# First FFN matrix as 2 x 2 blocks in seven products, six FFN phases, the residual in a DRAM scratch

## The chip, the core and the metric

The kernel runs on one core of one Trainium2 chip. The metric is the device time in microseconds (us) of one execution. Engines: TensorE (PE) multiplies, VectorE (DVE) and ScalarE (ACT) work element by element, GpSimd (POOL) builds masks, SyncE (SP) issues the transfers (DMA).

## What is computed

One layer of a hybrid encoder on 640 rows (512 of a prompt, 128 of eight samples) of 1024 columns in fp32: three token mixers on one normalised input, an attention to a memory, and a SwiGLU feed-forward part (FFN). The change is in the last.

```python
def swiglu(h, w_in, w_out):                    # h: rows x 1024, w_in: 1024 x 5632, w_out: 2816 x 1024
    g, u = jnp.split(h @ w_in, 2, axis=-1)
    return (jax.nn.silu(g) * u) @ w_out

h = rmsnorm(x, p['norm_ffn_pre'][l])
x = x + rmsnorm(swiglu(h, p['w_ffn_in'][l], p['w_ffn_out'][l]), p['norm_ffn_post'][l]).astype(x.dtype)
```

## The kernel before

Each fp32 operand of a large product is split into two parts (`split`): h, a cast by ACT to the type fp32r, and l, the rest, a subtraction by DVE. A product then is three matmuls, h by h, h by l and l by h, for each 128 of the contraction; they add up in one PSUM bank. Weights go through `ring`: a raw slot (three of them, `load_raw`), an h slot and an l slot (four of each). The slots have the size of the widest chunk, 4 x 278 columns. PSUM has eight banks, two for each of the tags g, t, z and o.

The order of the work on each engine is made by a planner from the priority in the program's text and from what is ready; the program only says what depends on what.

The stages in order: first norm; natural projections (`proj_nat`, seven chunks of 276 or 278 columns, the first two as rows arrive, three as fill of the stick-breaking attention, two as fill of the gated linear attention); that attention; gates and branch projections (`branch`, 320 columns); output projection with residual and next norm (`ProjD`, class with `start` for the first 512 columns and `finish` for the rest); memory attention; its output projection (`xo`, the same class); FFN.

`ProjD.finish` takes the tiles of 128 rows in turn: products, square sum, residual X, norm (`normed`, into a buffer of its own), and two tiles later the transposes (`done`). The last two calls of `done` are returned as `behind`. For `xo` they write fT_h and fT_l, the activations of the FFN transposed: 1024 channels by 640 rows.

The FFN (`ffn_phase`) has two phases of 11 x 128 hidden channels. A unit (`ffn_unit`, `ffn_load`) is 128 gate and the matching 128 up channels: 8 contraction tiles x 3 products for each, first for 384 rows, then for 256 (PARTS). ACT applies Silu to the gate's bank, DVE multiplies with the up's bank, and the result is split into ga or gb. In the first phase the first two units run their 384-row halves first, with `behind[0]` and `behind[1]` after them, and then their 256-row halves. After the 11 units come the products with the second matrix (L1199 to L1201), 512 columns at a time, for five tiles of rows; phase 0 copies the banks to Y, phase 1 adds Y and does the last norm, the residual and the stores (`finish`, L1217 to L1235).

Of the kernel before, what the change touches and what calls it, by code (L numbers as in the profile page):

```python
# [33 lines left out]
def tile_hybrid_stream_step(  # L34
# [27 lines left out]
    # ---------------------------------------------------------------- helpers  # L62
# [56 lines left out]
    def gemm_nat(ps, xh, xl, t0, slots, c0, cw, late=None, mid=None):  # L119
        """one tile of rows by cw columns"""  # L120
# [9 lines left out]
    def gemm_T(ps, slots, c0, xh, xl, t0, n, late=None):  # L130
        """128 columns by n rows, transposed"""
# [40 lines left out]
    def transposed(xn):  # L172
        """8 blocks of 128 columns, transposed, in two banks"""
# [13 lines left out]
    def normed(wpool, src, gain, bufs=2):  # L187
        """rmsnorm of 128 natural rows, by halves of the columns"""
        xn = wpool.tile([P, D], F32, tag="xn", bufs=bufs, name="xn")
# [33 lines left out]
    # ---------------------------------------------------------------- first norm  # L223
# [3 lines left out]
    widths = [276] * 5 + [278] * 2  # L227
# [21 lines left out]
    # products that keep the clock of the tensor engine up until the first rows are there  # L249
# [26 lines left out]
    # masks (functions of the shapes alone)  # L276
# [43 lines left out]
    # ---------------------------------------------------------------- pools of the mixer phase  # L320
# [24 lines left out]
    # natural projections: v of the stick-breaking heads, then q, k, low-rank input, v, gate of the linear attention  # L345
# [16 lines left out]
    # the first two chunks tile by tile, as the rows arrive  # L362
# [3 lines left out]
    # ---------------------------------------------------------------- projection u, pooling branch  # L366
# [21 lines left out]
    # pooling branch  # L388
# [36 lines left out]
    # pool state of the prompt (last 15 tokens) and of the samples (last 15 of 16 tokens)  # L425
# [13 lines left out]
    # q, k of the stick-breaking heads (transposed), v (natural), low-rank gate input  # L439
# [13 lines left out]
    # new keys and values of the stick-breaking heads  # L453
# [14 lines left out]
    # ---------------------------------------------------------------- stick-breaking attention  # L468
# [10 lines left out]
    def stick(z, t, m, n):  # L479
        """exp(z - sum of t over this and the later keys), m blocks of n keys"""  # L480
# [17 lines left out]
    def sb_prompt_a(i, hs):  # L498
        """weights of the heads hs for the queries of tile i, transposed"""
# [128 lines left out]
    # ---------------------------------------------------------------- gated linear attention  # L628
# [6 lines left out]
    def gla_prep(i):  # L635
        """transposed q, k, decay sums, and decayed keys of tile i"""
# [11 lines left out]
        # log decay (times tau)  # L648
# [12 lines left out]
        # running sums, transposed; remaining sums, natural  # L661
# [21 lines left out]
    def gla_main(i, pre, S):  # L683
# [6 lines left out]
        # attention inside the tile  # L690
# [5 lines left out]
        for hh in levels:  # L696
            nb = 64 // hh
            nk = P - hh  # no key is later than this
# [23 lines left out]
        # queries against the state  # L722
# [48 lines left out]
        # norm per head, output gate  # L771
# [18 lines left out]
    for c in range(5, 7):  # L790
        proj_nat(c)
# [9 lines left out]
    # ---------------------------------------------------------------- gates and branch projections  # L801
# [46 lines left out]
    # ---------------------------------------------------------------- output projection of the mixer  # L848
# [7 lines left out]
    class ProjD:  # L856
        """X += rmsnorm(x @ w) * gain, by tiles of rows: start(i) the first half of the columns, finish() the rest;
        done(i, rmsnorm(X) * gain2) for each tile of rows,
        two tiles behind; the last two calls are returned"""
# [17 lines left out]
        def finish(self, wpool, gain2, done):  # L877
            self.ws = load_w512(self.w2d, 512, 512, self.name + "1")
            xns = []
            for i in range(NT):  # L880
                self.unit(i, 1, (lambda: done(i - 2, xns[i - 2])) if i > 1 else None)
# [3 lines left out]
                for cs in (slice(0, 512), slice(512, D)):  # L885
                    nc.vector.scalar_tensor_tensor(X[:, i, cs], self.Y[:, i, cs], r, X[:, i, cs], ALU.mult, ALU.add)
                xns.append(normed(wpool, X[:, i, :], gain2, 3))
            return [lambda i=i: done(i, xns[i]) for i in (NT - 2, NT - 1)]
# [16 lines left out]
    # ---------------------------------------------------------------- cross-attention  # L905
# [6 lines left out]
    def proj_q():  # L912
        """all transposed products of the weight chunks; the first two run by groups of rows, as those arrive"""
# [50 lines left out]
    def softmax(ps, n):  # L964
        """n blocks of 256 columns of ps, normalised, into SBUF"""
# [13 lines left out]
    def xs_load(b):  # L979
        """cached keys of sample b, transposed, and values"""  # L980
# [48 lines left out]
    # keys and values of the prompt's memory  # L1029
# [48 lines left out]
    # the samples, between the products for the prompt's memory  # L1078
# [14 lines left out]
    # the prompt, between the products of the output projection  # L1093
# [22 lines left out]

    fpool = open_pool("fpool")
    nx = open_pool("nx", "right")
# [11 lines left out]
    def open_fw():  # L1130
        fw = open_pool("fw", "right")
        return fw, gain_tile(fw, norm_ffn_post, "gpost")

    fw = g_post = None

    def ffn_phase(ph):
        nonlocal fw, g_post
        ga_h = hpool.tile([P, KT, TOK], F32R, tag="th", name="ga_h")
        ga_l = hpool.tile([P, KT, TOK], F32R, tag="tl", name="ga_l")

        def gt(k):
            return (ga_h[:, k], ga_l[:, k]) if k < 8 else (gb_h[:, k - 8], gb_l[:, k - 8])
        def ffn_load(k):
            c0 = (ph * 11 + k) * P
            return load_w8(w1, [(c0, P), (FF + c0, P)], f"f{ph}_{k}", None)

        def ffn_unit(k, ws, half):
            dh, dl = gt(k)
            t0, n = PARTS[half]
            sl = slice(t0, t0 + n)  # L1150
            pg = bank([P, n], "g", "pg")
            gemm_T(pg, ws, 0, fT_h, fT_l, t0, n, 1 if ph == 0 and k < 2 else None)
            s = fpool.tile([P, PARTS[0][1]], F32, tag="sl", bufs=3, name="s")[:, 0:n]
            nc.scalar.activation(s, pg, AF.Silu)  # L1154
            pu = bank([P, n], "t", "pu")
            gemm_T(pu, ws, P, fT_h, fT_l, t0, n, 1 if ph == 0 and k < 2 else None)
            nc.vector.tensor_tensor(s, pu, s, ALU.mult)  # L1157
            split(dh[:, sl], dl[:, sl], s)
        w0 = [ffn_load(k) for k in range(2)]
        for half in range(2):  # L1160
            for k in range(2):
                ffn_unit(k, w0[k], half)
                if ph == 0 and half == 0:
                    behind[k]()
            if ph == 0 and half == 0:
                nx.release()
                nw.release()
                fw, g_post = open_fw()
        gb_h = fw.tile([P, 3, TOK], F32R, tag="gb_h", name="gb_h")
        gb_l = fw.tile([P, 3, TOK], F32R, tag="gb_l", name="gb_l")  # L1170
        for k in range(2, 11):
            ws = ffn_load(k)
            for half in range(2):
                ffn_unit(k, ws, half)
# [110 lines left out]
```

## Time and profile before

| | us |
|---|---|
| median of 3 runs | 1336.32 |
| lowest and highest | 1333.74, 1336.38 |
| span of the profiled execution | 1332.9 |
| PE busy | 1313.9 (99%) |
| DVE busy | 629.3 (47%) |
| ACT busy | 541.5 (41%) |

The median is 3.4 us above the span of the profiled execution. A duration in a row is that of one instruction from start to end; PE's instructions overlap, so their distance from start to start is shorter than their duration. Rows with x4 or x8 put that many consecutive instructions together.

### The profile page before, as it was taken

The numbers are of one execution on the slowest core, as the hardware profiler recorded it, in microseconds if no ns is written. First come the engines' busy times: TensorE is split into PE (matmuls) and PEld (weight loads), VectorE is DVE, ScalarE is ACT, GpSimd is POOL, SyncE is SP. The second block draws the span as 40 slices with busy tenths as digits, with TensorE's granted clock in tenths as the row PEclk, the third lists the DMA queues.
The fourth block names the chain that finished last, engine by engine and source line by source line (L and its number), as shares of the span: only waits on it lengthen the run. The fifth ranks groups of instructions, "written<-read, shape, count | busy, mean of one in ns | idle before, by whom it ended". The sixth has DMA issues, their size and how long they took to land.

```text
span 1332.9 us, 21503 instructions
## 1 busy us (share of the span) xinstructions
PE 1313.9 (99%) x8754; PEld 1194.7 (90%) x8754; DVE 629.3 (47%) x1242; ACT 541.5 (41%) x1087; POOL 41.3 (3%) x162
## 2 busy tenths in 40 slices
PE   9999999999999999999999999999999999999997
PEld 8998678988999999979988878899999889999986
DVE  6434775485587454547444434742322112322235
ACT  5324665454353454435444523642222222322222
POOL 2001111001000000000000000000000000000000
PEclk9999999999999999999999999999999999999999
DMA  7324231202412222422368821232222223232212
GB/s 233 112 77 128 82 97 49 60 1 66 116 30 68 84 88 75 144 94 95 127 227 296 270 79 33 70 105 64 84 75 72 72 73 86 64 95 64 75 52 79
DMA packets 134296, 128.65 MB, mean 97 GB/s; under 512 B 15670, under 2 KB 116613, under 8 KB 134197
## 3 DMA queue, kind: packets, MB, share of 16 engines
q1 hardware_dynamic: 133909, 126.98, 30.7%
q8 instruction: 69, 1.13, 0.3%
q0 software_dynamic: 288, 0.29, 0.1%
q14 instruction: 30, 0.25, 0.1%
HBM read 119.10 MB, written 8.15 MB: 95 GB/s over the span
## 4 chain that ended last, share of the span: by engine, by line
PE 93%; DVE 3%; DMA 2%; ACT 1%; issue 0%; SPq 0%; POOL 0%; DVEq 0%; ACTq 0%
PE ps_g L114 12%; PE pu L114 12%; PE pg L114 12%; PE ps_d L114 8%; PE ps_n L114 7%; PE ps_xq L114 4%; PE ps_b L114 4%; PE acc L1201 4%; PE acc L1199 4%; PE acc L1200 4%; PE ps_qk L114 3%; PE pl L718 2%; PE ps_xk L114 2%; PE ps_xv L114 1%; PE z L505 1%; PE xo L1074 1%
## 5 line engine op out<-in xcount | busy, mean ns | idle before, releaser
L1157 DVE TENSOR_TENSOR s<-pu,s 128x384 f32<-128x384 f32 (+1 forms) x44 | 21.5, 488 | 125.2 <-PE pu L114 125.2
L1199 PE MATMUL acc<-wh_o,ga_h 128*128 128x512 f32 (+1 forms) x168 | 64.5, 384 | 0.0
L1201 PE MATMUL acc<-wh_o,ga_l 128*128 128x512 f32 (+1 forms) x168 | 64.4, 384 | 0.0
L1200 PE MATMUL acc<-wl_o,ga_h 128*128 128x512 f32 (+1 forms) x168 | 64.3, 382 | 0.0
L89 DVE TENSOR_TENSOR wl_o<-raw_o,wh_o 128x1024 fp32r<-128x1024 f32 (+1 forms) x24 | 27.2, 1135 | 77.7 <-ACT wh_o L83 77.5
L1154 ACT ACTIVATE s<-pg 128x384 f32<-128x384 f32 (+1 forms) x44 | 19.3, 439 | 89.6 <-PE pg L114 89.6
L813 ACT ACTIVATE sgm<-ps_g 128x320 f32<-128x320 f32 x48 | 21.0, 437 | 66.0 <-PE ps_g L114 65.9
L83 ACT CAST wh_o<-raw_o 128x1024 fp32r<-128x1024 f32 (+1 forms) x24 | 23.5, 978 | 49.8 <-PE acc L1201 36.7
L143 ACT CAST ga_h<-s 128x384 fp32r<-128x384 f32 (+1 forms) x32 | 14.7, 459 | 63.2 <-DVE s L1157 63.2
L1201 PEld LDWEIGHTS acc<-wh_o,ga_l 128*128 128x128 f32 x168 | 31.5, 188 | 6.8
L1200 PEld LDWEIGHTS acc<-wl_o,ga_h 128*128 128x128 f32 x168 | 31.6, 188 | 6.7
L1199 PEld LDWEIGHTS acc<-wh_o,ga_h 128*128 128x128 f32 x168 | 31.5, 188 | 6.5
L718 PEld LDWEIGHTS pl<-X 96*120 96x120 f32 (+6 forms) x256 | 28.9, 181 | 6.4 <-issue 3.7
L814 DVE TENSOR_SCALAR sgm<-sgm 128x320 f32<-128x320 f32 x48 | 15.5, 325 | 40.4 <-ACT sgm L813 40.3
L718 PE MATMUL pl<-X 96*120 96x64 f32 (+6 forms) x256 | 30.5, 263 | 2.8 <-DVE X L714 2.7
L114 PE MATMUL ps_d<-wh_xo,oT_h 128*128 128x512 f32 x80 | 32.4, 405 | 0.0
L114 PE MATMUL ps_d<-wh_mix,mT_h 128*128 128x512 f32 x80 | 31.9, 398 | 0.0
L114 PE MATMUL ps_d<-wl_xo,oT_h 128*128 128x512 f32 x80 | 31.7, 396 | 0.0
L114 PE MATMUL ps_d<-wh_xo,oT_l 128*128 128x512 f32 x80 | 31.6, 396 | 0.0
L114 PE MATMUL ps_d<-wl_mix,mT_h 128*128 128x512 f32 x80 | 31.6, 395 | 0.0
L114 PE MATMUL ps_d<-wh_mix,mT_l 128*128 128x512 f32 x80 | 31.4, 392 | 0.0
L815 ACT ACTIVATE sgm<-sgm 128x320 f32<-128x320 f32 x48 | 22.5, 469 | 15.8 <-DVE sgm L814 15.7
(1207 smaller groups left out, 4442.1 us busy)
## 6 DMA issues: line engine op xcount, KB each, us to landing
raw_o<-in_w_ffn_out_dram SPq DMA_DIRECT2D x20, 512.0 KB, 3.8
kc<-in_cache_mem_k_dram SPq DMA_DIRECT2D x16, 512.0 KB, 4.8
vc<-in_cache_mem_v_dram SPq DMA_DIRECT2D x16, 512.0 KB, 5.4
raw_mix<-in_w_mix_out_dram SPq DMA_DIRECT2D x8, 512.0 KB, 4.2
raw_xo<-in_w_xo_dram SPq DMA_DIRECT2D x8, 512.0 KB, 6.2
kn<-in_cache_sb_k_dram SPq DMA_DIRECT2D x24, 128.0 KB, 2.5
vn<-in_cache_sb_v_dram SPq DMA_DIRECT2D x24, 128.0 KB, 2.7
out_dram<-X SPq DMA_DIRECT2D x10, 256.0 KB, 2.0
```

What stands on the lines that cost most here:

```text
L83: nc.scalar.copy(wh, raw)
L89: (eng or nc.vector).tensor_tensor(wl, raw, wh.bitcast(F32), ALU.subtract)
L114: ins = nc.tensor.matmul(ps, a, b, start=(j == 0), stop=(j == len(todo) - 1))
L718: nc.tensor.matmul(pl[0:nk, h], X[:, h, 0:nk], mv_, start=True, stop=True)
L813: nc.scalar.activation(s, ps, AF.Exp, scale=-1.0)
L814: nc.vector.tensor_scalar(s, s, 2.0 ** 63, None, ALU.min)
L815: nc.scalar.activation(s, s, AF.Ln, bias=1.0)
L1154: nc.scalar.activation(s, pg, AF.Silu)
L1157: nc.vector.tensor_tensor(s, pu, s, ALU.mult)
L1199: nc.tensor.matmul(ps, ah, wh[:, kk, lo:hi], start=(first and kk == 0), stop=False)
L1200: nc.tensor.matmul(ps, ah, wl[:, kk, lo:hi], start=False, stop=False)
L1201: nc.tensor.matmul(ps, al, wh[:, kk, lo:hi], start=False, stop=(last and kk == nk - 1))
```

## The change

The first matrix, the activations and the result of a unit are taken as 2 x 2 blocks: the contraction in halves of 512, the rows in halves of 320 (each with 64 sample rows and two prompt tiles: new order of the columns of fT), the channels in gate and up. The four result blocks come from seven block products (P1 to P7) instead of eight, each 4 contraction tiles x 3 matmuls x 320 columns. For this, sums and differences of activation blocks (S_h, S_l; once, `s_prep`) and of weight blocks (`sums`; for each unit) are made on DVE and split as before, and sums of products are made in PSUM (X, Z) and by DVE and ACT behind it. The first unit of all stays plain (`plain_unit`).

The FFN has six phases (4, 3, 3, 4, 4, 4 units). The second matrix is loaded as 128 x 1024 pieces, one for each unit. Y takes the place of X; X holds the normalised rows and their fp32 transposes first. The residual goes to a DRAM scratch `xd` after the memory attention and comes back in the last phase. In the blocks marked manual PE keeps the order of the text. `xo.finish` takes the tiles as 4, 0, 1, 2, 3. The raw slots are four, and the natural projections run in eight chunks of 242 columns, so that no slot is wider than 1024 elements.

```diff
-        raw = ring.tile([P, nk, sum(c for _, c in cols)], F32, tag="raw", bufs=3, name=f"raw_{name}")
+        raw = ring.tile([P, nk, sum(c for _, c in cols)], F32, tag="raw", bufs=4, name=f"raw_{name}")
...
-    widths = [276] * 5 + [278] * 2
+    widths = [242] * 8
...
-    for c in range(5, 7):
+    for c in range(5, 8):
...
     def after_xo(i, xn):
-        split_T(transposed(xn), fT_h, fT_l, i * P)
-    behind = xo.finish(nx, g2, after_xo)
+        for b, tp in enumerate(transposed(xn)):
+            ks = slice(4 * b, 4 * b + 4)
+            nc.scalar.copy(x32(i)[:, ks, :], tp)
+            src = tp.rearrange("p k (two c) -> p k two c", two=2) if i == 4 else tp
+            split(cols(fT_h[:, ks], i), cols(fT_l[:, ks], i), src)
+    behind = xo.finish(None, g2, after_xo, (4, 0, 1, 2, 3), True)
+    for i in (4, 0, 1, 2, 3):
+        nc.sync.dma_start(xd[i], Y[:, i, :])
...
+    def s_prep(a, b, o):
+        w = a.shape[-1]
+        nc.vector.tensor_tensor(b[:, 4:8], b[:, 0:4], b[:, 4:8], addop)
+        nc.vector.tensor_tensor(b[:, 0:4], a[:, 0:4], b[:, 0:4], sub)
+        nc.vector.tensor_tensor(a[:, 0:4], b[:, 4:8], a[:, 0:4], sub)
+        nc.vector.tensor_tensor(a[:, 4:8], a[:, 4:8], a[:, 0:4], sub)
+        split(S_h[:, 0:8, o:o + w], S_l[:, 0:8, o:o + w], b)
+        split(S_h[:, 8:16, o:o + w], S_l[:, 8:16, o:o + w], a)
...
+    AH = {"P1": ((fT_h, fT_l), 0, 0), "P2": ((fT_h, fT_l), 4, 0), "P4": ((fT_h, fT_l), 4, H2),
+          "P7": ((S_h, S_l), 0, 0), "P5": ((S_h, S_l), 4, 0), "P6": ((S_h, S_l), 8, 0), "P3": ((S_h, S_l), 12, 0)}
+    class Unit:
...
+        def sums(self):
...
+            nc.vector.tensor_tensor(ta[:, 1], rb[:, 0], ra[:, 1], sub)
+            nc.vector.tensor_tensor(ta[:, 0], ra[:, 1], ra[:, 0], sub)
+            nc.vector.tensor_tensor(ra[:, 1], ta[:, 1], ra[:, 0], addop)
+            nc.vector.tensor_tensor(self.t4[:, 0], rb[:, 1], ra[:, 1], sub)
+        def parts(self, which):
+            src, names = {"ra": (self.ra, ("P1", "P6")), "ta": (self.ta, ("P5", "P7")),
+                          "rb": (self.rb, ("P3", "P2")), "t4": (self.t4, ("P4",))}[which]
...
+            split(h, l, src)
...
+        def mm(self, nm, ps, start, stop=True):
+            (ah, al), k0, c0 = AH[nm]
+            bh, bl = self.w[nm]
+            todo = []
+            for kk in range(4):
+                a, b = ah[:, k0 + kk, c0:c0 + H2], al[:, k0 + kk, c0:c0 + H2]
+                todo += [(bh[:, kk], a), (bh[:, kk], b), (bl[:, kk], a)]
...
+        def p1(self):
+            self.X = bank([P, H2], "g", "fX")
+            self.mm("P1", self.X, True)
...
+            nc.scalar.copy(self.p1s, self.X)
+        def p6(self):
+            self.mm("P6", self.X, False)
...
+            nc.scalar.copy(self.u2, self.X)
+        def p2(self):
+            self.Yb = bank([P, H2], "t", "fY")
+            self.mm("P2", self.Yb, True)
...
+            nc.vector.tensor_tensor(self.s[:, 0], self.Yb, self.p1s, addop)
+            nc.scalar.activation(self.s[:, 0], self.s[:, 0], AF.Silu)
+        def p5(self):
+            self.Zb = bank([P, H2], "t", "fZ")
+            self.mm("P5", self.Zb, True)
...
+            nc.scalar.copy(self.p5s, self.Zb)
+        def p7(self):
+            self.mm("P7", self.X, False)
+            nc.vector.tensor_tensor(self.c[:, 1], self.X, self.p5s, addop)
+        def p3(self):
+            self.mm("P3", self.Zb, False)
+            nc.vector.tensor_tensor(self.c[:, 0], self.Zb, self.u2, addop)
+        def p4(self):
+            self.mm("P4", self.X, False)
+            nc.scalar.activation(self.s[:, 1], self.X, AF.Silu)
+            nc.vector.tensor_tensor(self.s, self.s, self.c, ALU.mult)
+            g_split(self.k, self.s)
...
+    PHASES = (4, 3, 3, 4, 4, 4)
...
+    s_mid = [lambda: (behind[0](), s_prep(x32(4)[:, :, 0:64], x32(4)[:, :, 64:128], 0)),
+             lambda: (behind[1](), s_prep(x32(0), x32(2), 64), s_prep(x32(1), x32(3), 192))]
...
+        if ph == 0:
+            plain_unit(0, 0, s_mid)
...
+        with tc.manual_schedule(engines={mybir.EngineType.PE}):
+            for j, u in enumerate(us):
...
+                if j == 0 and ph == 0:
+...
+                if j == 0:
+...
+                u.p6()
+                if nx_:
+                    nx_.sums()
+                    nx_.parts("ra")
+                u.p5()
+                if nx_:
+                    nx_.parts("ta")
+                u.p2()
+                u.p7()
+                if nx_:
+                    nx_.parts("rb")
+                    nx_.p1()
+                u.p3()
+                if nx_:
+                    nx_.parts("t4")
+                u.p4()
...
+            early = nk - 2
+            for k in range(early):
+                for i in range(NT):
+                    out_mms(i, k, wo[k], 0, 512, acc[i][2], k == 0, False)
...
+                nxt.sums()
+                for w_ in ("ra", "ta", "rb", "t4"):
+                    nxt.parts(w_)
```

For the first unit of the blocks PE's order is another: p1, p2, p1 of the next unit, p6, p5, p7, p3, p4 in the first phase, and p1, p5, p2, p6, p1 of the next unit, p7, p3, p4 in the others. In the last phase each tile of rows takes its remaining first-half products, all of its second half and its norm in turn.

## Rows read from the trace of the kernel before

**Rows 1.** Head of the page: span, and busy time of each engine.
```profile
span 1332.9 us, 21503 instructions
...
PE 1313.9 (99%) x8754; PEld 1194.7 (90%) x8754; DVE 629.3 (47%) x1242; ACT 541.5 (41%) x1087; POOL 41.3 (3%) x162
```
**Rows 2.** The page's chain that ended last, by engine.
```profile
PE 93%; DVE 3%; DMA 2%; ACT 1%; issue 0%; SPq 0%; POOL 0%; DVEq 0%; ACTq 0%
```
**Rows 3.** Windows, the FFN: length, busy us (instructions) per engine, clock, DMA.
```profile
861.00:1326.00 465.00, 464.59 (x2819) 435.97 (x2817) 147.21 (x224) 132.36 (x214) 0.00 (x0) 1.00 0.25 76
```
**Rows 4.** Timeline, PE (start, duration, operation): third unit, its second half, second matrix.
```profile
891.01 0.34 PE L114 MATMUL pg<-fT_h,wh_f_2a 128*128 128x384 f32 x1
...
899.43 0.28 PE L114 MATMUL pg<-fT_h,wh_f_2a 128*128 128x256 f32 x1
...
1017.70 0.39 PE L1199 MATMUL acc<-wh_o,ga_h 128*128 128x512 f32 x1
```
**Rows 5.** Timeline, PE: first and 34th of a run of 320-column products.
```profile
507.24 0.31 PE L114 MATMUL ps_g<-hT_h,wh_gc1a 128*128 128x320 f32 x1
...
512.09 0.31 PE L114 MATMUL ps_g<-hT_h,wh_gc1a 128*128 128x320 f32 x1
```
**Rows 6.** Timeline, PE: first and 22nd of a run of 512-column products.
```profile
1041.43 0.39 PE L1199 MATMUL acc<-wh_o,ga_h 128*128 128x512 f32 x1
...
1046.30 0.39 PE L1199 MATMUL acc<-wh_o,ga_h 128*128 128x512 f32 x1
```
**Rows 7.** Timeline, PE: first and last of 24 products with 276 columns.
```profile
43.81 0.29 PE L114 MATMUL ps_n<-wh_n1a,hT_h 128*128 128x276 f32 x1
...
46.74 0.29 PE L114 MATMUL ps_n<-wh_n1b,hT_l 128*128 128x276 f32 x1
```
**Rows 8.** Timeline, ACT and DVE: a cast and two splits in the last stage.
```profile
1294.54 1.05 ACT L83 CAST wh_o<-raw_o 128x1024 fp32r<-128x1024 f32 x1 [3.25 <-PE acc L1201]
...
1295.62 1.23 DVE L89 TENSOR_TENSOR wl_o<-raw_o,wh_o 128x1024 fp32r<-128x1024 f32 x1 [3.07 <-ACT wh_o L83]
1302.21 0.69 DVE L89 TENSOR_TENSOR wl_o<-raw_o,wh_o 128x512 fp32r<-128x512 f32 x1 [5.36 <-ACT wh_o L83]
```
**Rows 9.** Two tiles of the branches: ns min/median/max of passes over 320 columns.
```profile
L813 ACT ACTIVATE sgm<-ps_g x48: 428/438/441, 265.8 to 555.5; 128x320 f32<-128x320 f32 x48
...
L823 DVE TENSOR_TENSOR sgm<-ps_b,sgm x32: 480/492/493, 410.0 to 558.1; 128x320 f32<-128x320 f32 x32
```
**Rows 10.** Timeline, start of the FFN: PE, then DVE, then ACT.
```profile
868.86 0.60 PE L179 MATMUL tp<-ident,xn 128*128 128x128 f32 x4
...
879.56 0.72 PE L114 MATMUL pg<-fT_h,wh_f_0a 128*128 128x256 f32 x4
...
865.83 1.40 DVE L198 SCALAR_TENSOR_TENSOR xn<-X,t,g 128x512 f32<-128x512 f32 x2
...
874.90 1.42 DVE L198 SCALAR_TENSOR_TENSOR xn<-X,t,g 128x512 f32<-128x512 f32 x2
...
870.10 1.28 ACT L151 ACT_TABLE_LOAD   x1
```
**Rows 11.** Windows, memory attention: length, busy us per engine, granted clock, DMA.
```profile
765.00:770.00 5.00, 3.31 (x21) 1.92 (x19) 1.97 (x8) 2.54 (x10) 0.00 (x0) 0.98 0.96 311
770.00:775.00 5.00, 5.00 (x26) 3.27 (x23) 1.42 (x5) 0.37 (x1) 0.00 (x0) 0.68 0.48 154
```
**Rows 12.** Timeline, PE: plain fp32 products with 127, 64 and 128 weight columns.
```profile
270.74 1.07 PE L718 MATMUL pl<-X 96*127 96x64 f32 x8
275.28 0.68 PE L718 MATMUL pl<-X 96*64 96x64 f32 x8
...
794.46 1.03 PE L1058 MATMUL xs<-mkT,qT 128*128 128x256 f32 x4
```
**Rows 13.** Timeline, tail: DVE's last step of a tile, PE's last product.
```profile
1318.80 1.42 DVE L1234 SCALAR_TENSOR_TENSOR X<-Y,t,X 128x512 f32<-128x512 f32 x2
...
1325.59 0.28 PE L1201 MATMUL acc<-wh_o,gb_l 128*128 128x256 f32 x1
```

More of the change, by code (lines that the diff above doesn't have):

```diff
@@ L185, in split_T, with normed @@
             split(dst_h[:, 4 * b:4 * b + 4, t0:t0 + P], dst_l[:, 4 * b:4 * b + 4, t0:t0 + P], tp)
-    def normed(wpool, src, gain, bufs=2):
-        xn = wpool.tile([P, D], F32, tag="xn", bufs=bufs, name="xn")
+    def normed(wpool, src, gain, bufs=2, xn=None):
+        if xn is None:
+            xn = wpool.tile([P, D], F32, tag="xn", bufs=bufs, name="xn")
         halves = (slice(0, 512), slice(512, D))
@@ L885, in finish @@
                 for cs in (slice(0, 512), slice(512, D)):
[L886 to L888 removed]
+                    nc.vector.scalar_tensor_tensor(res[:, i, cs], self.Y[:, i, cs], r, X[:, i, cs], ALU.mult, ALU.add)
+                xns[i] = normed(wpool, res[:, i, :], gain2, 3, X[:, i, :] if in_y else None)
+            return [lambda i=i: done(i, xns[i]) for i in order[-2:]]
     nw = open_pool("nw", "right")
@@ new lines, in tile_hybrid_stream_step, with cols, x32 @@
+    xd = tc.dram_tile([NT, P, D], F32, name="xd")
+    def cols(t, i):
+        if i == 4:
+            return t.rearrange("p k (two c) -> p k two c", two=2)[:, :, :, 0:64]
+        c0 = (64, 192, H2 + 64, H2 + 192)[i]
+        return t[:, :, c0:c0 + P]
+    def x32(i):
+        return X[:, i, :].rearrange("p (k c) -> p k c", c=P)
+    def after_xo(i, xn):
+        for b, tp in enumerate(transposed(xn)):
[3 more added lines that the diff above has]
+            split(cols(fT_h[:, ks], i), cols(fT_l[:, ks], i), src)
@@ new lines, in tile_hybrid_stream_step @@
+    behind = xo.finish(None, g2, after_xo, (4, 0, 1, 2, 3), True)
+    for i in (4, 0, 1, 2, 3):
+        nc.sync.dma_start(xd[i], Y[:, i, :])
+    nw.release()
+    ypool.release()
+    Y = X
+    fw = open_pool("fw", "right")
+    g_post = gain_tile(fw, norm_ffn_post, "gpost")
+    ga_h = fw.tile([P, 4, TOK], F32R, name="ga_h")
+    ga_l = fw.tile([P, 4, TOK], F32R, name="ga_l")
+    w1, w2 = w_ffn_in[0], w_ffn_out[0]
+    S_h = hpool.tile([P, 16, H2], F32R, tag="th", name="S_h")
+    S_l = hpool.tile([P, 16, H2], F32R, tag="tl", name="S_l")
@@ new lines, in tile_hybrid_stream_step @@
+    sub, addop = ALU.subtract, ALU.add
+    def s_prep(a, b, o):
[6 more added lines that the diff above has]
+        split(S_h[:, 8:16, o:o + w], S_l[:, 8:16, o:o + w], a)
@@ new lines, in gt, with g_split, rows_of @@
+    def gt(k):
+        return [(t[:, k, 0:512], t[:, k, 512:TOK]) for t in (ga_h, ga_l)]
+    def g_split(k, s):
+        (ph_, sh_), (pl_, sl_) = gt(k)
+        two = lambda t: t.rearrange("p (t c) -> p t c", t=2)
+        split(two(ph_), two(pl_), s[:, :, 64:H2])
+        split(two(sh_), two(sl_), s[:, :, 0:64])
+    def rows_of(g, i):
+        return g[1] if i == 4 else g[0][:, i * P:(i + 1) * P]
+    AH = {"P1": ((fT_h, fT_l), 0, 0), "P2": ((fT_h, fT_l), 4, 0), "P4": ((fT_h, fT_l), 4, H2),
+          "P7": ((S_h, S_l), 0, 0), "P5": ((S_h, S_l), 4, 0), "P6": ((S_h, S_l), 8, 0), "P3": ((S_h, S_l), 12, 0)}
@@ new lines, in plain_unit @@
+    def plain_unit(n, k, mids):
+        ws = load_w8(w1, [(n * P, P), (FF + n * P, P)], "f0")
+        st = fpool.tile([P, 2, H2], F32, tag="s", bufs=1, name="s")
+        s = st.rearrange("p t c -> p (t c)")
+        for part, (t0, w) in enumerate(PARTS):
+            sl = slice(t0, t0 + w)
+            pg = bank([P, w], "g", "pg")
+            gemm_T(pg, ws, 0, fT_h, fT_l, t0, w, 1)
+            nc.scalar.activation(s[:, sl], pg, AF.Silu)
+            if part == 0:
+                mids[0]()
+            pu = bank([P, w], "g", "pu")
+            gemm_T(pu, ws, P, fT_h, fT_l, t0, w, 1)
+            nc.vector.tensor_tensor(s[:, sl], pu, s[:, sl], ALU.mult)
+            if part == 0:
+                mids[1]()
+        g_split(k, st)
@@ new lines, in w2_load, with w2_parts, out_mms @@
+    def w2_load(n):
+        return load_raw(w2, n, 1, [(0, D)], f"o{n}")
+    def w2_parts(raw):
+        return split_w(raw, "o")
+    def out_mms(i, k, wp, c0, w, ps, first, last):
+        wh, wl = wp[0], wp[1]
+        gh, gl = gt(k)
+        ah, al = rows_of(gh, i), rows_of(gl, i)
+        nc.tensor.matmul(ps, ah, wh[:, 0, c0:c0 + w], start=first, stop=False)
+        nc.tensor.matmul(ps, ah, wl[:, 0, c0:c0 + w], start=False, stop=False)
+        nc.tensor.matmul(ps, al, wh[:, 0, c0:c0 + w], start=False, stop=last)
```

238 lines of the change are left out of this document (138 added, 100 removed).

## The prediction, made before the changed kernel ran

> **What bounds the kernel now.** I read the page's head first: TensorE (PE) is busy 99% of the 1332.9 us span, VectorE (DVE) 47%, ScalarE (ACT) 41% [rows 1]. PE's busy share counts pipelined instructions, so the next view is the chain of work that ended last: 93% of it is PE [rows 2]. The reader should see there that a transfer or another engine ends almost nothing. The table by windows then says it for the stage that changes: from 861 to 1326 us, the whole feed-forward part (FFN), PE is busy 464.59 of 465 us at full granted clock, DVE 147.21, ACT 132.36 [rows 3]. So in this stage the time is the number of products times the distance between their starts, and the timeline gives that distance. Nine gate/up units start at 891.01 and the first product with the second matrix at 1017.70: 126.69 / 9 = 14.08 us each [rows 4]. Products with 320 columns lie 0.147 us apart (33 of them from 507.24 to 512.09) [rows 5], those with 512 columns 0.232 us (21 in 4.87 us) [rows 6], those with 276 columns 0.1274 us (23 distances in 2.93 us) [rows 7].
>
> **The block products (the gain).** A unit of before is 48 products of 384 and 48 of 256 columns. A unit of after is seven block products of 4 x 3 matmuls with 320 columns: 84 x 0.147 = 12.35 us. One of 22 units stays plain. Before: 22 x 14.08 = 309.8. After: 21 x 12.35 + 14.08 = 273.4. **-36.4 us**, all of it on the path, since PE alone binds there [rows 3, 4, 5]. The second matrix keeps its 660 products at 0.232 us, 153.1 us, whatever the number of phases [rows 6]. The rule that speaks against such a change is in the Trainium skill, "TensorE: Matmul & The Clock Gate", section "Back-to-back issue gap": in a stream of weight loads and matmuls it gives about 81 ns at 128 columns and 131 ns at 512, so that narrower instructions gain little. A line through these, an estimate from that page, gives 114, 98 and 106 ns for 384, 256 and 320 columns and a saving of 27 us instead of 36 (1324 at the end). This trace contradicts it with 232 ns at 512 columns [rows 6]; so the row decides and the rule gets no chance of its own.
>
> **The added elementwise work, in a running unit.** DVE: four sums of weight blocks of 512 elements at 0.69, splits of three 1024s at 1.23 and of one 512 at 0.69, three adds of 320 at 0.49, one product of 640 (between 0.69 and 1.23, taken 0.82), the split of the result about 0.94: 2.8 + 4.4 + 1.5 + 0.8 + 0.9 = 10.4 us [rows 8, 9]. That is 84% of 12.35 us; in the stretch of before it is 147.21 / 465 = 32% [rows 3]. ACT: three casts at 1.05, five passes of 320 at 0.44 and some 1.5 us of smaller casts, about 7 us [rows 8, 9]. Both fit under PE. What counts are two handoffs. P7 adds onto the PSUM bank of P6 and must wait until ACT has copied it; P5 and P2 (3.5 us) lie between. P4 adds onto it again and must wait for DVE's add of P7; P1 of the next unit and P3 (3.5 us) lie between. With a split of 1.23 us in front, the add of 0.49 ends some 2 us after P7. So 0 to 0.4 us per unit; I take **+1** in all (0 to 8), nearer to zero because the cover is almost twice the need.
>
> **Six phases.** The last unit of a phase has no successor, so between P7 and P4 only P3 (1.76 us) covers 0.49 plus what is in front of it; the first unit of a phase has only P1 of the next between P6 and P7. At 0.3 us, eleven places give 3. At the end of a phase the last result goes ACT, DVE, ACT, DVE (0.44 + 0.82 + 0.6 + 0.69, with handoffs some 3.5 us), while the products of the earlier result tiles run: 15 x 0.232 = 3.5 us each, one or two of them [rows 6]. Slots for the next phase's weights come free 10.4 to 3.5 us ahead of need. I take **+2** (0 to 6). The loads keep their bytes, and DMA has 2% of the chain [rows 2].
>
> **The start of the FFN: the largest new wait.** Before, the first halves of two units (2 x 8.4 us) stand between the last projection and the first products that need the last rows, those with 256 columns at 879.56, and there is no gap [rows 3, 10]. After, there is one plain unit: its first half (both 384-column parts) ends at 868.86, where the transposes of the last tile but one stand now. The normalised last rows are there only at 874.90 + 1.42 = 876.3, because ACT reloads its table for logarithm and exponential between (1.28 us at 870.10) [rows 10]. Behind that come two transposes, two new copies into X and two casts on ACT, so about 878 to 879: PE has a hole of 8 us. P1 and P2 of the next unit and P1 of the one after (5.3 us) need only the first rows and could fill it, but then they are missing later. S, the sums of activations, needs on DVE about 13.5 us (two calls of 4 x 0.69 + 2 x 1.23, one half as wide) and the next unit's weights 7.1 [rows 8]. Counted from 865.83, where DVE takes up the last tile but one, these 20.6 us end at 886; with the rows' own work I put S at 886 to 890, where PE would arrive at 884 to 889. So **+8** (3 with the hole filled, 13 with S late). An idle stretch of PE also costs clock: after a stretch with 3.31 of 5 us busy the granted clock is 0.68 in the next five, that is 1.2 GHz for part of them and 1.6 us lost [rows 11]: **+1.5** (0 to 3). The residual's five stores to DRAM and their loads 440 us later lie beside PE work; the loads must land before the first tile's end, some 11 us into the last phase. Zero, with 0 to 3 us if they are late.
>
> **The natural projections.** Seven chunks of 276 or 278 columns become eight of 242: 840 products at 0.1274 to 0.129 are 107.4 us. The distances at 276 and at 384 columns (48 from 891.01 to 899.43, 0.1754 each) give a slope of 0.444 ns per column, so 0.1123 at 242 [rows 4, 7]. A floor by the weight load lies at the same place: with 127 weight columns and only 64 moving ones the records lie (1.07 - 0.29) / 7 = 0.11 us apart, with 64 weight columns (0.68 - 0.29) / 7 = 0.056 [rows 12]. 960 x 0.112 = 107.5: **0** (-3 to +3, for the fill moves from the attention stage to the next one; the fourth raw slot may gain a little).
>
> **The tail.** A tile of the last stage takes PE 18 x 0.232 = 4.2 us, where it was 21 x 0.232 = 4.9 before. DVE needs per tile four passes of 0.69, two of 0.71 (1.42 together) and five small ones: about 4.8 us [rows 8, 13]. It falls behind by up to 0.6 us a tile, and the 7.3 us from the last product (1325.59) to the end grow: **+1.5** (0 to 3).
>
> **Sum.** 1332.9 - 36.4 + 1 + 2 + 8 + 1.5 + 0 + 1.5 = 1310.5 for the profiled execution [rows 1]. The median of the runs, 1336.32, is 3.4 above its span, so **1314 us**.
>
> **The rivals.** A: every wait is covered. Then only -36.4 is left, 1300 us. For it: PE shows no gap before from 861 on, and P1 and P2 can go ahead. Against it: the last rows arrive at 876.3 and the plain unit has 14.1 us of work, of which 8.4 do not need them [rows 10].
> B, slower: DVE's queue, not PE, sets the unit. The adds of P7 and P3 stand in one queue with splits that wait for ACT's casts and for weight slots. If two further splits of 1.23 are in front of the add, it ends 4.5 to 5.6 us after P7 and P4 waits up to 2 us. From 1.1 us per unit on, the forecast's gain of 22 us is gone; with 2 us in 21 units the time is 1314 + 42 = 1356. For it: 84% load on a queue that has waits in it. Against it: 2 us of slack per unit, and covers of 3.5 us.
> C, much slower: 242 columns. No three-part product in the trace is narrower than 256 columns, so no row excludes that such products are treated in another way there. The nearest dearer rows are the plain fp32 products: four records of 256 columns take 1.03 us, (1.03 - 0.40) / 3 = 0.21 us apart, and each product has two records, 0.42 us [rows 12]. At 242 columns this is 0.40 - 0.112 = 0.285 us more on 960 products, 274 us: 1588. It decides as soon as the width falls under some threshold between 242 and 256. Against it: between 512 and 276 columns the distance follows one line, and the weight floor is reached only at 242.
> That the change does not do what it says is no case here: the code writes out 1764 + 96 products where it wrote out 2112.
>
> **How the numbers follow.** Forecast 0.61, A 0.20, B 0.11, C 0.06, others 0.02. The predicted time is the forecast's, 1314. Its own bounds reach from 1304 (hole filled) to 1330 (most terms near their upper ends); with A, 1300 to 1330 holds about 0.8. About 0.2% (2.7 us) is what a measurement of this kernel can tell from no change. Faster by more: 0.81. Within: 0.03 (B near its break-even). Slower: 0.16 (the rest of B, C, others).
>
> **What would show it.** Distance of the new 320-column products: 0.147 us, 12.35 us per unit from P4 to P4. PE gaps of some microseconds between 868 and 890, and a clock under 1.00 behind them; almost none later. DVE at about 80% in the gate/up phases with PE still at 99%. Products of 242 columns 0.112 us apart, or 0.4 if C is right. From the last product to the end 8 to 10 us. The prediction is wrong if PE waits for DVE or ACT in each unit, if the 242-column products lie further apart, or if the start costs less than 3 us.

## The result, and the profile after

The changed kernel takes **1375.82 us** (median of four runs, 1375.24 to 1376.74) against 1335.72 for the kernel before in the same session: ratio 1.031, 95% interval 1.029 to 1.033. The forecast was 1314, range 1300 to 1330. The head of the page, PE's clock in 40 slices, and the chain that ended last (the views of [rows 1, 2]):

```profile
span 1373.7 us, 21638 instructions
...
PE 1306.3 (95%) x8601; PEld 1179.8 (86%) x8601; DVE 782.4 (57%) x1468; ACT 619.4 (45%) x1224; POOL 38.9 (3%) x162
...
PEclk8998888999999999999999999997999999999998
...
PE 85%; DVE 6%; ACT 4%; DMA 2%; issue 2%; POOL 0%; SPq 0%; DVEq 0%; ACTq 0%; POOLq 0%
```

The FFN is the place of the change, but the first thing to read is where the low digits of the clock stand: in slices 4 to 7, some 103 to 240 us, long before the FFN. The first products of the FFN start at 915.00 us; before, they started at 860.4. So 54.6 us are lost ahead of it. The FFN itself takes 1373.7 - 915.0 = 458.7 us instead of 1332.9 - 860.4 = 472.5, a gain of 13.8. The difference of the spans is 54.6 - 13.8 = 40.8 us.

**Where the 55 us went.** The view by windows, PE's products into ps_n alone (the natural projections): length, busy us and count, granted clock, DMA. First the kernel before, then the changed one, for the stick-breaking attention and for what follows it:

```profile
110.00:230.00 120.00, 64.71 (x419) 1.00 0.34 97
230.00:320.00 90.00, 23.59 (x183) 1.00 0.15 42
```
```profile
110.00:230.00 120.00, 27.44 (x115) 0.80 0.24 70
230.00:320.00 90.00, 71.03 (x605) 0.98 0.24 69
```

A chunk is 120 products. Before, three chunks and a bit are fill between the attention's short steps, and the clock stays at 1.00. After, one chunk is, the clock falls to 0.80, and the other five chunks run in a row behind the attention, where nothing hides them. PE's last product of the attention, before and after:

```profile
221.17 0.27 PE L592 MATMUL tp_on<-ident,on 128*128 128x128 f32 x1
...
232.60 0.33 PE L593 MATMUL tp_on<-ident,on 128*128 128x128 f32 x1
```

The first products of the attention (into z) start at 107.36 us before and at 112.63 after. So the attention takes 113.8 us with 380 products of fill in it, and 120.0 us with 119: taking the fill out made it no shorter. Behind it stand 220 products of ps_n before, which end 32.1 us later, and 601 after, which end 76.4 us later. The three places together make the loss: 5.3 us up to the attention (the same 240 products, the first of the next stage at 52.3 us instead of 47.0), 6.2 in it and 44.3 behind it.

The fill was not late. The timeline of the changed kernel has chunk 3 (DVE's last split of its weights, then PE's first product with them):

```profile
113.16 1.16 DVE L89 TENSOR_TENSOR wl_n3b<-raw_n3b,wh_n3b 128x968 fp32r<-128x968 f32 x1
...
232.88 0.28 PE L114 MATMUL ps_n<-wh_n3a,hT_h 128*128 128x242 f32 x1
```

The weights lay ready for 118 us, while PE was busy for only 98.76 of the 120 us of the window (118.83 before): chunk 3 stands behind the attention in the order that was laid down for PE. Nor are the products dear on the chip. In the same kernel:

```profile
269.98 0.28 PE L114 MATMUL ps_n<-wh_n5b,hT_h 128*128 128x242 f32 x1
...
273.05 0.28 PE L114 MATMUL ps_n<-wh_n5b,hT_h 128*128 128x242 f32 x1
```

27 distances in 3.07 us: 0.1137 us, where the prediction had 0.1123.

**The FFN.** Two units apart, on the timeline (first product of P2 in the last two units):

```profile
1310.95 0.31 PE L1234 MATMUL fY<-fT_h,wh_f 128*128 128x320 f32 x1
...
1323.25 0.31 PE L1234 MATMUL fY<-fT_h,wh_f 128*128 128x320 f32 x1
```

12.30 us a unit against 14.08 [rows 4]. And what PE waited for in the whole FFN, 915 to 1360 us (engine and line, releaser: us in total, times, longest):

```profile
PE tp L179 <- DVE X L199: 5.2, 1, 5.2
PE fX L1234 <- ACT wh_f L143: 3.6, 1, 3.6
PE fY L1234 <- DVE wl_f L144: 2.6, 1, 2.6
PE acc L1304 <- DVE y L1409: 0.8, 1, 0.8
PE fX L1234 <- DVE wl_f L144: 0.4, 1, 0.4
PE pg L114 <- ACT fT_h L143: 0.3, 1, 0.3
```

Every one but the 0.8 (at 1357 us) lies between 924 and 952 us, at the start. The other nineteen block units and the five changes of phase have none. The clock falls with the waits (windows of the same kernel: busy us of PE, PEld, DVE, ACT, POOL, granted clock, DMA):

```profile
925.00:935.00 10.00, 4.63 (x20) 4.26 (x21) 9.02 (x18) 9.32 (x15) 0.00 (x0) 0.67 0.22 66
...
950.00:955.00 5.00, 4.64 (x17) 4.24 (x18) 0.98 (x1) 0.43 (x1) 0.00 (x0) 0.50 0.36 105
```

**The tail.** The timeline of ACT, DVE and PE at the end (the views of [rows 13]):

```profile
1329.64 1.28 ACT L1390 ACT_TABLE_LOAD   x1
1330.93 1.28 ACT L1271 ACT_TABLE_LOAD   x1
1332.23 0.44 ACT L1271 ACTIVATE s<-fX 128x320 f32<-128x320 f32 x1
...
1344.35 1.28 ACT L151 ACT_TABLE_LOAD   x1
...
1345.96 1.28 ACT L152 ACT_TABLE_LOAD   x1
...
1358.57 0.28 PE L1306 MATMUL acc<-wh_o,ga_l 128*128 128x256 f32 x1
...
1368.60 0.22 DVE L155 SCALAR_TENSOR_TENSOR t<-y,m 128x1 f32<-128x1 f32 x1 [1.85 <-ACT y L152]
```

L1390 loads the table set that holds both the logarithm and the exponential, once for the whole last stage. In the changed kernel it was laid down one instruction ahead of the last Silu (L1271), which loads its own set over it. So each of the five tiles of rows loads two tables of 1.28 us for L151 and L152, and DVE waits. From the last product to the end it is 15.1 us instead of 7.3. That a change of set costs a load of 1283 ns, the Trainium skill says too ("ScalarE activation tables: per-element evaluation and per-set limits", section "What a function is on this engine"), and the rows agree with 1.28 us. Its section "Table sets in the compiler and the runtime" says that the compiler's back end places the loads for the greedy longest run. The rows don't look like that: one set serves both functions, as L1390's own does in the runs below, and two were loaded in turn. What placed the loads of this kernel, no run shows.

### The profile page after: what moved, and what is told of

Read it like the earlier page. It is cut to its first block, busy times and chain, and to the rows that moved or that the text cites. A ratio compares the mean times of both kernels' runs of the same rounds, so it can differ in the third digit from the quotient of the medians.

```text
span 1373.7 us, 21638 instructions
## 1 busy us (share of the span) xinstructions
PE 1306.3 (95%) x8601; PEld 1179.8 (86%) x8601; DVE 782.4 (57%) x1468; ACT 619.4 (45%) x1224; POOL 38.9 (3%) x162
## 4 chain that ended last, share of the span: by engine, by line
PE 85%; DVE 6%; ACT 4%; DMA 2%; issue 2%; POOL 0%; SPq 0%; DVEq 0%; ACTq 0%; POOLq 0%
PE ps_g L114 13%; PE fX L1234 11%; PE ps_d L114 7%; PE ps_n L114 7%; PE fZ L1234 5%; PE ps_b L114 4%; PE ps_xq L114 4%; PE acc L1305 3%; PE acc L1304 3%; PE acc L1306 3%; PE fY L1234 3%; PE ps_qk L114 3%; PE pl L719 2%; PE ps_xv L114 2%; PE ps_xk L114 1%
## 5 line engine op out<-in xcount | busy, mean ns | idle before, releaser
L1234 PE MATMUL fX<-fT_h,wh_f 128*128 128x320 f32 x168 | 52.6, 313 | 3.6 <-ACT wh_f L143 3.6
L1234 PE MATMUL fX<-fT_h,wl_f 128*128 128x320 f32 x168 | 52.7, 313 | 0.4 <-DVE wl_f L144 0.4
L1234 PE MATMUL fX<-fT_l,wh_f 128*128 128x320 f32 x168 | 52.5, 312 | 0.0
L1234 PE MATMUL fX<-S_h,wh_f 128*128 128x320 f32 x168 | 52.2, 311 | 0.0
L1234 PE MATMUL fX<-S_h,wl_f 128*128 128x320 f32 x168 | 52.2, 311 | 0.0
L1234 PE MATMUL fX<-S_l,wh_f 128*128 128x320 f32 x168 | 52.0, 310 | 0.0
L1234 PE MATMUL fZ<-S_h,wl_f 128*128 128x320 f32 x168 | 51.9, 309 | 0.0
L1234 PE MATMUL fZ<-S_h,wh_f 128*128 128x320 f32 x168 | 51.9, 309 | 0.0
L1234 PE MATMUL fZ<-S_l,wh_f 128*128 128x320 f32 x168 | 51.9, 309 | 0.0
L143 ACT CAST wh_f<-ra 128x1024 fp32r<-128x1024 f32 x21 | 22.1, 1051 | 47.7 <-PE acc L1306 36.4
L1406 DVE TENSOR_TENSOR X<-acc,X 128x512 f32<-128x512 f32 x40 | 26.7, 689 | 18.4 <-PE acc L1306 18.4
```

The costliest lines, as they stand in the source:

```text
L1234: nc.tensor.matmul(ps, w_, m_, start=(start and j == 0), stop=(stop and j == 11), skip_group_check=True)
L1406: nc.vector.tensor_tensor(dst, ps, dst, addop)
```

## The experiments

### The width of the natural chunks

Theory W: the widths are enough for the 55 us, through the order that the planner lays down. The four raw slots, or another part of the change, are the rival. First the widths alone, in the kernel before:

```diff
-    widths = [276] * 5 + [278] * 2
+    widths = [242] * 8
...
-    for c in range(5, 7):
+    for c in range(5, 8):
```

> The kernel before with one part of the change alone: its natural projections in eight chunks of 242 columns instead of seven of 276 and 278. Theory W (the width): the order laid down for TensorE then holds only one narrow chunk (some 120 products) between the products of the stick-breaking attention instead of three chunks (360), the rest follow back to back behind it, and the time rises by the 55 us that separate the two traces ahead of the FFN (254 to 309 us at the last natural product): 1385 to 1393 us. Theory R (the ring of four raw slots, or anything else that the change does, carries those 55 us): no more than the 120 extra products cost, 1336 to 1340 us.

1390.49 us (1386.05 to 1392.43), ratio 1.041 (1.039 to 1.044), 55 us above the kernel before: the widths alone make the whole of it. Then two twins, two columns apart (`[254] * 7 + [158]` and `[256] * 7 + [144]`, the loop as above):

> The kernel before with its natural projections as seven chunks of 254 columns and one of 158; its twin has 256 and 144. Theory W in its sharp form (a product narrower than 256 columns counts as a dear one when the order is laid down, whatever it takes on the chip): like the 242-column form, 1380 to 1393 us, while a 254-column product still takes about 0.118 us from start to start on the chip. Rival S (narrower products are gradually worse, on the chip or in the order): within 3 us of its twin of 256 columns.

> The kernel before with its natural projections as seven chunks of 256 columns and one of 144, two columns more per chunk than its twin. Theory W: three chunks lie between the products of the stick-breaking attention again, 1334 to 1342 us, some 50 us under the twin. Rival S: within 3 us of the twin, wherever that lies.

254 columns: 1385.80 us, ratio 1.037 (1.033 to 1.041). 256 columns: 1339.60 us, ratio 1.003 (1.002 to 1.005). The same windows of ps_n, 254 and then 256 columns:

```profile
110.00:230.00 120.00, 24.51 (x105) 0.83 0.25 70
230.00:320.00 90.00, 75.56 (x616) 0.96 0.24 65
```
```profile
110.00:230.00 120.00, 64.15 (x437) 1.00 0.32 91
230.00:320.00 90.00, 33.17 (x286) 1.00 0.13 39
```

Two columns move nearly three chunks out of the window, and 46 us with them. A gradual effect (rival S) can't do that. On the chip the 254-column products are not dear (first and 31st of a run, 30 distances in 3.54 us, 0.118 us):

```profile
239.86 0.28 PE L114 MATMUL ps_n<-wh_n3a,hT_h 128*128 128x254 f32 x1
...
243.40 0.28 PE L114 MATMUL ps_n<-wh_n3a,hT_h 128*128 128x254 f32 x1
```

The step lies between 254 and 256 columns, in the order of the instructions and not in the products. Why the planner steps there, the traces don't show; that it counts a narrower product of this type as several times dearer would explain it, since one chunk of that price fills the attention as three did, but it was only argued. Now the changed kernel with chunks of 256 columns or more:

```diff
-    widths = [242] * 8
+    widths = [256] * 6 + [400]
...
+        if p1_ - p0_ > 256:
+            return load_w512(w_in2, cols[0][0], cols[0][1], f"n{c}")
         return load_w8(w_in2, cols, f"n{c}")
...
-    for c in range(5, 8):
+    for c in range(5, 7):
```

> The changed kernel with six chunks of 256 columns and a last one of 400 (its weights in four slots of two k tiles), all else as changed. Theory W: the 55 us ahead of the FFN come back and the 14 us that the FFN gained stay: 1375.8 - 55 = 1318 to 1324 us, ratio 0.987 to 0.991. Theory R (the four raw slots or another part of the change holds the order back): 1370 us or more. The FFN alone still starts late and ends late as in the changed kernel (hole of 5 us behind the first products, two table loads per tile of rows at the end).

1321.80 us (1320.12 to 1326.77), ratio 0.990 (0.987 to 0.993): faster than before by 1.0%, with the FFN as changed. Its windows of ps_n:

```profile
110.00:230.00 120.00, 64.11 (x438) 1.00 0.32 92
230.00:320.00 90.00, 27.07 (x164) 0.94 0.13 39
```

So W stands, from both sides, and the raw slots are out.

### The two ends of the FFN

All that follows starts from that kernel. At the tail, the load is tied behind the last Silu:

```diff
-            nc.scalar.activation(self.s[:, 1], self.X, AF.Silu)
+            self.silu = nc.scalar.activation(self.s[:, 1], self.X, AF.Silu)
...
-            tc.keep_in_program_order(nc.scalar.preload_act_table_set("natural_log_exp_and_others"))
+            with tc.issue_after(us[-1].silu.ins):
+                nc.scalar.preload_act_table_set("natural_log_exp_and_others")
```

At the start, two plain units instead of one (both 384-row halves first, `behind[0]` and `behind[1]` after them, as before the change):

```diff
-            plain_unit(0, 0, s_mid)
-            us = us[1:]
+            plain_units(s_mid)
+            us = us[2:]
```

> The changed kernel with the wide chunks (1321.8 us), and the load of the table set that holds both Ln and Exp tied behind the last Silu instead of one instruction ahead of it. Theory T (the ten table loads of 1.28 us in the last stage hold up VectorE, which ends 14.5 us behind the last product instead of 7.3): the end comes 5 to 8 us earlier, 1314 to 1317 us, and the last stage holds no table load any more. Rival D (VectorE's own passes or the output transfers of six phases set the end): less than 2 us, 1320 us or more.

> The changed kernel with the wide chunks (1321.8 us), and two plain units of eight block products ahead of the block units instead of one, as the kernel before had at its start. Theory C (cover): the hole of 5.2 us before the last normalised rows and the waits of 2.6 and 3.6 us for the weight parts of the first two block units go, some 2 us of half clock with them, and the second plain unit costs 14.08 - 12.35 = 1.7 us: 1308 to 1314 us. Rival S (the sums of the activations and their parts on VectorE and ScalarE are late whatever TensorE does meanwhile): the holes move behind the second unit, 1320 to 1325 us.

> Both at once. If the two ends are independent the gains add: 1300 to 1308 us, ratio to the kernel before 0.974 to 0.980. If the earlier start is given back later (a queue that catches up), less than the sum.

Tail alone: 1315.92 us, ratio 0.986 (0.984 to 0.988). Start alone: 1312.32, 0.985 (0.982 to 0.988). Both: 1306.53, 0.980 (0.977 to 0.982). Against 0.990 that is 0.4% and 0.5%, and 1.0% together: they add. Each landed inside its expected range, though single runs of one version lie up to 8.5 us apart. The traces tell the parts better: from the first product of the FFN to the end of the span it is 458.8 us with the wide chunks alone, 452.1 with the tail mend, 448.4 with the start mend and 441.7 with both, so 6.7, 10.4 and 17.1 us less. The code ahead of the FFN is the same in the four, and its first product starts at 859.8 to 866.2 us: much of the scatter lies there. The timeline of the tail mend shows the load behind the Silu, none after it, and PE's last product:

```profile
1279.41 0.44 ACT L1273 ACTIVATE s<-fX 128x320 f32<-128x320 f32 x1 [0.85 <-PE fX L1236]
1279.86 1.28 ACT L1393 ACT_TABLE_LOAD   x1
...
1306.47 0.28 PE L1308 MATMUL acc<-wh_o,ga_l 128*128 128x256 f32 x1
```

From there to the end of the span (1315.9) it is 9.4 us: 5.7 less than 15.1. The start mend leaves these waits of PE in the FFN:

```profile
PE fX L1236 <- ACT wh_f L143: 2.3, 1, 2.3
PE acc L1306 <- DVE y L1411: 0.8, 1, 0.8
PE pg L114 <- ACT fT_h L143: 0.7, 1, 0.7
PE fX L1236 <- DVE wl_f L144: 0.7, 1, 0.7
```

4.5 us instead of the 12.9 of the changed kernel. What is left asks for the second block unit's weights in third place, by an order written out for the first unit alone. The next version takes that order away:

```diff
-                if j == 0 and ph == 0:
-                    u.p1()
-                    u.p2()
...
-                    continue
                 if j == 0:
                     u.p1()
                     u.p5()
```

> The version of both mends, with the first block unit's products in the order that the first unit of every later phase has (first, fifth, second, sixth, then the next unit's first) instead of the next unit's first product in third place. In the twin that third product waits 2.4 us for its weight part and 0.7 us for the lower part. If those waits come from asking for the next unit's weights too early, 1.5 to 3 us go: 1303 to 1306 us, ratio 0.976 to 0.979. If the fifth product now waits instead for the sums of the activations, nothing changes: 1305 to 1309 us.

**1301.73 us** (1299.43 to 1305.44), ratio 0.976 (0.973 to 0.978), the fastest version of the study. Against 0.980 of its twin that is 0.4%, some 5 us, a little more than the 1.5 to 3 expected; from the first product of the FFN to the end it is 437.6 us in the trace, 4.1 less than the twin. PE's waits in its whole FFN:

```profile
PE fZ L1236 <- DVE wl_f L144: 0.8, 1, 0.8
PE pg L114 <- ACT fT_h L143: 0.7, 1, 0.7
```

### What the seven products are worth, and how far VectorE is from the bound

All 22 units plain, with the wide chunks and the tail mend (`for u in us: plain_unit(u.n, u.k, ...)` in place of the block units):

> The changed kernel with the wide chunks and the table load behind the last Silu, and with all 22 units as eight plain block products (the sums of activations still made, those of weights not). Theory P (seven products for eight are worth 14.08 - 12.35 = 1.73 us a unit on the chip, as the distances of the products say): 21 x 1.73 = 36 us more than its twin with block units, less the 8 to 12 us of waits at the twin's start that plain units don't have: 24 to 36 us above the twin, 1338 to 1352 us. Rival G (the gain is given back to VectorE's longer queue and to the hand-overs): less than 15 us above the twin.

1348.05 us, ratio 1.011 (1.008 to 1.013): 32 us above its twin (1315.92), theory P. Its own hole at the start is longer, 8.9 us (PE's first transposes of the last rows wait for VectorE), and it has no other wait in the FFN but one of 0.3.

Then the slots, with the kernel's old widths (`widths = [276] * 5 + [278] * 2`, raw `bufs=3`) in the version of both mends, and VectorE made slower (the first weight sum five and nine times; the result is the same):

```diff
-            nc.vector.tensor_tensor(ta[:, 1], rb[:, 0], ra[:, 1], sub)
+            for _ in range(5):
+                nc.vector.tensor_tensor(ta[:, 1], rb[:, 0], ra[:, 1], sub)
```

> The version of both mends, with the kernel's old widths (five chunks of 276, two of 278) and three raw weight slots instead of four, which is what leaves room for them. Ahead of the FFN the old chunks should give what the wide ones give, within 4 us. Theory N (the fourth slot is not needed): 1303 to 1311 us. Rival F (the seven products need the fourth slot, since a unit holds three of them while the next one's load waits): the loads land one unit late and each unit waits 1 to 2 us: 1320 to 1345 us.

> The version of both mends with 2.8 us more of VectorE work in each block unit (the first weight sum made five times, 4 x 0.69 us). In 12 us of running units VectorE is busy for 8.7 to 9.2 us. Theory M (it sets the unit only where its sum reaches the 12.35 us of the seven products): 8.9 + 2.8 = 11.7, no more than 4 us slower, 1306 to 1311 us. Rival B (its order of work already meets the products' due times closely): 10 us slower or more, 1317 us and up.

> The same with 5.5 us more (eight repeats). Theory M: 8.9 + 5.5 = 14.4 us against 12.35, 2.1 us a unit wherever one block unit follows another (14 of the 20; the first of a phase is made ready under the output projection): 20 to 40 us slower than the twin, 1327 to 1347 us. If VectorE is off the path altogether: within 5 us of the twin.

Three slots: 1310.94 us, ratio 0.982 (0.980 to 0.984), 4 us above the twin: the running units don't need the fourth slot, since their only wait is one of 0.3 us. At the start PE waits 4.8 us for a weight part of the second block unit (2.4 in the twin). The old widths also make the second matrix dearer, by some 3 us (see the last section). With 2.8 us more on VectorE: 1314.11, ratio 0.985 (0.983 to 0.987), 7.6 us above the twin, between the two expectations. The running units have no wait; PE's only waits are again at the start, where they grow from 3.8 to 9.0 us:

```profile
PE fX L1237 <- ACT wh_f L143: 6.5, 1, 6.5
```

The 2.4 us that these 5.2 leave of the 7.6 are within what single runs differ by; from the first product of the FFN to the end the two traces differ by 5.5 us (447.2 and 441.7). With 5.5 us more: 1366.58, ratio 1.024 (1.021 to 1.026), 60 us above the twin. PE's longest waits, and then a window over two units of that run:

```profile
PE fX L1237 <- ACT wh_f L143: 29.5, 14, 8.6
```
```profile
1188.29:1222.69 34.40, 30.51 (x181) 29.45 (x181) 30.04 (x46) 12.93 (x23) 0.00 (x0) 0.90 0.21 62
```

The 14 units that follow another wait, as theory M has it. But the loss is 60 us, not 20 to 40. A unit takes 17.2 us in this window. VectorE is busy for 15.0 of them, and not 14.4; in the rest it waits itself (in the two units 2.0 us for products, 1.4 for a weight load, 0.8 for casts), and PE's waits also take clock (0.90). What each of these costs was not taken apart. So VectorE's queue does set the unit from some point between 2.8 and 5.5 us a unit on.

## Why the prediction was wrong

By its own steps, in us against the span of 1332.9:

| step | predicted | measured |
|---|---|---|
| block products | -36.4 | -37.4: 21 x (14.08 - 12.30) |
| second matrix | 0 | about -3: 660 x (0.232 - 0.227), see the last section |
| handoffs in the units | +1 | 0 |
| six phases | +2 | 0 |
| start of the FFN, with its clock | +8 and +1.5 | about +19: the FFN's -13.8 less the other rows |
| natural projections, all ahead of the FFN | 0 (-3 to +3) | +54.6 |
| tail | +1.5 | +7.8 |

**The step that failed is that of the natural projections.** It priced the products rightly (0.112 us against 0.1137) and then let the fill "move from the attention stage to the next one" for nothing. That was nearly the same price in all, but their place was not free: as fill they cost the path nothing, since the attention took 113.8 us with 380 of them and 120.0 with 119, and behind the attention they cost all that they take, 601 products in 76.4 us where 220 had taken 32.1. That is 44.3 of the 54.6 us; 6.2 are the attention's own, which stands still more and runs at a lower clock, and 5.3 lie ahead of it, in the first norm's stage, where the order changed too. The prediction looked at the width only as a price on the chip. Rival C had the threshold between 242 and 256 columns, but as slow products with 1588 us, and the products of 254, 242 and 144 columns took 0.118, 0.114 and 0.112 us. None of the cases held "the order changes", though the order is made by a planner from the sizes in the program. With the chunks at 256 columns the time is 1321.8, inside the range of 1300 to 1330.

**The start was too small by half.** The hole was 5.2 us where 8 were forecast, so the arrival of the last rows was right. But the waits for the weight parts of the first two block units (2.6 and 3.6 us) came on top, and with half clock the three cost about 19. The bound of 13 us with "S late" was too low for another reason than S, for which PE never waits. The prediction let DVE's queue of S and of one unit's weight parts end at 886 us, 25.6 behind the first product of the FFN. In the trace it ends at 945.87, 30.9 behind, and the weight sums of the second block unit, which are not in the forecast, start only then:

```profile
945.18 0.69 DVE L144 TENSOR_TENSOR wl_f<-t,wh_f 128x512 fp32r<-128x512 f32 x1
...
946.63 0.68 DVE L1211 TENSOR_TENSOR ta<-rb,ra 128x512 f32<-128x512 f32 x1
```

Two plain units are the cover, as e6_two_plain showed.

**The tail** had the right reason at the right size for what it counted: with the load mended it is 9.4 us, 2.1 more than before, against +1.5. It missed that the load of the table set had moved ahead of the last Silu, 5.7 us. That is again an order that came out otherwise than the program's text suggests.

**The parts that held:** the distance of the 320-column products and so the value of the block products (the plain twin is 32 us slower), the cover of the handoffs (VectorE is busy for 75% of the running units from 1140 to 1165 us, 18.80 of 25, where 84% were forecast), the phases, the residual's way through DRAM (its loads are issued from 1328.7 us on, the first use is at 1348.9, and no wait of PE for them is in the trace). The row also held against the rule of the Trainium skill ("TensorE: Matmul & The Clock Gate", section "Back-to-back issue gap"): by an estimate from that page the block products were worth 27 us, by the row 36, and 37 came. Rival A's 1300 us, every wait covered, is nearly what the last version reaches, 1301.73; that is partly luck, since it has two plain units and a longer tail on the one side and the cheaper second matrix on the other. Rival B is not met: the units keep pace with 2.8 us more on VectorE, and not with 5.5.

## What to carry to other kernels

Where a planner orders the work, a change of a tile's size is also a change of the order: compare where the fill stands, by windows of its tile, before its price. What looks free because it is hidden is worth its whole time on the day it is not, and a stage that loses its fill can lose clock too (0.80 instead of 1.00 here). Tie down what must come last (a table load behind the last use of the old table), and give a new queue of preparations a plain piece of work in front to start behind.

## What the runs showed of the hardware

Products of 144 columns lie as close as those of 242. In the twin of 256 columns, whose last chunk has 144:

```profile
257.98 0.28 PE L114 MATMUL ps_n<-wh_n7a,hT_h 128*128 128x144 f32 x1
...
261.33 0.27 PE L114 MATMUL ps_n<-wh_n7a,hT_h 128*128 128x144 f32 x1
```

30 distances in 3.35 us, 0.1117 us, against 0.1137 at 242 columns; so there is a floor, near the 0.11 that the prediction drew from other rows [rows 12].

The same 512-column products took 0.2314 us where the ring's slots are 278 columns wide (21 distances in 4.86 us in the version with three slots, first pair; [rows 6] has 0.232) and 0.2267 us where they are 256 wide (21 in 4.76 us in the twin of 256 columns, second pair):

```profile
991.79 0.39 PE L1306 MATMUL acc<-wh_o,ga_h 128*128 128x512 f32 x1
...
996.65 0.39 PE L1306 MATMUL acc<-wh_o,ga_h 128*128 128x512 f32 x1
```
```profile
1039.99 0.39 PE L1199 MATMUL acc<-wh_o,gb_h 128*128 128x512 f32 x1
...
1044.75 0.39 PE L1199 MATMUL acc<-wh_o,gb_h 128*128 128x512 f32 x1
```

The code of these products is the same in the kernel before and in its twin of 256 columns, so what differs is the slots and where they lie: an h slot of 4 x 278 columns is 4448 bytes, one of 4 x 256 is 4096. The traces of the other runs agree for the second matrix, 0.2267 to 0.2270 us wherever the slots are 256 columns wide or less. But it is not the width alone. The first 172 of the 512-column products of the mixers' output projection (from 557 us on) lie 0.2333 us apart in the runs with the start mend alone and with 5.5 us more on VectorE, and 0.2289 in the other versions of the changed kernel with the same slots. What does it, the start of a slot in memory or something else, was not tried on its own.
